# Second norm applied to the feed-forward's products, the embeddings' projection moved inside heads five to seven, and the last output column in a bank of its own

## The chip, the cores and the metric

One Trainium2 chip, one of its cores. The metric is the device time of one execution in microseconds; the kernel before takes 1887.27 us (median of three runs, 1885.65 to 1888.17).

## The reference

One encoder layer on two requests (groups 0 and 1 here) of 512 tokens and 1024 channels each, float32, with shared weights:

```
h = rmsnorm(x, g_mix);  u = h @ w_in            # -> mLSTM, attention, merge gates
y_m = (sigmoid(o) * mlstm(...)) @ w_mo
q_rope = rope(q_r, cos, sin)                     # x1*cos - x2*sin, x1*sin + x2*cos
y_a = mla_attention(q_nope, q_rope, k_nope, k_rope, v) @ w_ao     # 8 heads
x = x + (g_m * y_m + g_a * y_a) @ w_out
h2 = rmsnorm(x, g_ffn)                           # the second norm: x * r * g_ffn, r one number a token
x = x + (silu(h2 @ w_gate) * (h2 @ w_up)) @ w_down
x = x + sigmoid(x @ w_ple_gate) * (p_l @ w_ple)  # p_l: the per-layer embeddings, 256 channels
return rmsnorm(x, g_final)
```

## The kernel before

Activations lie with channels on the 128 partitions and 512 tokens along the row, so a [128, 512] tile is one block of channels of one group. A float32 product is three TensorE matmuls in a reduced format: operand and weight are each split into a rounded high part (a cast on ScalarE) and the rest (a subtraction on VectorE, `lo_of`), and hi*hi, lo*hi and hi*lo are summed in one PSUM bank. So each weight block costs TensorE three matmuls of 512 columns per 128x128, ScalarE one cast and VectorE one subtraction.

The stages, in order: norm and projections, mLSTM (to about 560 us of the profiled execution), eight attention heads, each for both groups (575 to 864 us), the chain of the mLSTM's and the attention's output projections (864 to 1019 us), the output projection `w_out` with its residual (1019 to 1111 us), sixteen projections of the embeddings (1111 to 1135 us), the feed-forward (gate and up to about 1545 us, down to 1772 us), the embedding gate and the final norm.

**Products by `Seven`.** `w_mo`, `w_ao` and the three feed-forward matrices are multiplied for both groups at once in Strassen's way: seven products (P1, P2, P7, P6, P5, Q4, P3) of twelve matmuls each stand for eight. `Ops` (L839) makes the seven operands by sums of blocks (which engine adds is its third argument), `Seven.weights` (L915) makes the sums of the weights on the engine `adds`, `outputs` (L977) combines the banks, and `chain` (L953) interleaves the products of neighbouring pairs. `put` receives each finished block.

**Attention.** `attn_proj` (L769) projects queries and keys of a head out of the low-rank latents into the PSUM tag `pj` (2 buffers, L709); every second head it also turns the rotary part with `rope` (L741): one multiply by the cosines over all 128 partitions, four multiplies by the sines over 32 partitions each, which write to exchanged partitions, and an add. `attn` (L787) does scores, softmax, transposes and the product with the values. Between the heads stand the merge gates' projections (`BULK`) in heads one to four, and the preparation of the first operands of the `w_mo` chain (`HOPS`) in heads five to seven; in its sums P7 is subtracted on VectorE, the others on GpSimd (L1014).

**Second norm.** The output projection (L1123 to L1142) works off group 0's eight columns, then group 1's. Each column's sum of squares goes into `ss`; `sums` (L1099) adds them over the partitions on TensorE (tile `ssc`), `inv` makes 1/sqrt on VectorE (tiles `rv` to `rw`), `spread2` (L1113) spreads it over the partitions again with TensorE (tile `rbc`). `hn` (L1106) multiplies a block of x with gain and norm, and the feed-forward's operands are made of those. So for group 1 the operands can only be made when the last column has been summed; meanwhile TensorE does the sixteen projections of `emb` (L1155), six matmuls each, into tiles `em` and to DRAM.

**Order.** A scheduler with a model of time orders each engine's instructions, except where `pinned` is set (the last column and `emb` here, and the end). DMAs are issued from SyncE's queue (SP), in order; those of `Seven`'s weights from ScalarE's.

Of the kernel before, what the change touches and what calls it, by code (L numbers as in the profile page):

```python
# [62 lines left out]
def encoder_kernel(ctx: ExitStack, tc: tile.TileContext, a):  # L63
# [87 lines left out]
    V.tensor_scalar(out=hg, in0=cols[:, 24:32], scalar1=0.5, scalar2=None, op0=ALU.mult)  # L151

# [588 lines left out]
    def rope(src, nblk):  # L741
        n = 32 * nblk
        r = Q("tr", "rp")
        V.tensor_tensor(out=r[0:n], in0=src[0:n], in1=cos[0:n], op=ALU.mult)
        s = Q("tr", "rs")
        for i in range(nblk):
            o = i ^ 1
            V.tensor_tensor(
                out=s[32 * o : 32 * o + 32], in0=src[32 * i : 32 * i + 32], in1=sin[32 * i : 32 * i + 32], op=ALU.mult
            )  # L750
        V.tensor_tensor(out=r[0:n], in0=r[0:n], in1=s[0:n], op=ALU.add)
        return r
# [16 lines left out]
    def attn_proj(hd, g, wa):  # L769
        if hd % 2 == 0:  # L770
            r = rope(proj1(wa, lat["cq"][g], 2, 0, "pj"), 4)
# [181 lines left out]
    def chain(quads, head=False, look=4):  # L953
# [89 lines left out]
    z1d = [[dr.tile([P, T], F32, name=f"z1d{g}_{c}") for c in range(KD)] for g in range(G)]  # L1043
# [42 lines left out]
    banks("P3", dict(mm=5, tp=1, bc=2), mm="mm", tp="ssc", bc="rbc")  # L1086
# [38 lines left out]
    pp, wple = [], []  # L1125
    w = w8("out0")
    for c in range(KD):
        nxt = w8(f"out{c + 1}") if c < KD - 1 else None
        pinned[0] = c == KD - 1
        out_proj(1, c, w, {0: lambda: sums(0), 1: lambda: spread2(0)}.get(c))  # L1130
# [3 lines left out]
        if 2 <= c < 6:
            h2.need("P1", [c - 2])
            h2.need("P2", [c - 2])
        if c == 3:
            pp = [[split(load(a[f"p{g}"][k], OP, "ev"), OP, "h", "pl") for k in range(2)] for g in range(G)]
        if c == 5:
            st = [load(a["wple"][i // 2][:, i % 2 * T : i % 2 * T + T], OP, "ev") for i in range(4)]  # L1140
            wpn[0] = 2
            wple.append(wsplit(st[0]))  # L1142


    emd = [[dr.tile([P, T], F32, name=f"emd{g}_{c}") for c in range(KD)] for g in range(G)]
    todo = [(c, g) for c in range(KD) for g in range(G)]

    emn = [0]

    def em_tile():  # L1150
        sl_, tag = ((OP, "sg"), (EV, "ch"), (OP, "sg"), (EV, "bk"))[emn[0] % 4]
        emn[0] += 1
        return sl_(tag, "em")

    def emb(n):  # L1155
        for _ in range(n):
            c, g = todo.pop(0)
            while len(wple) < min(4, c // 2 + 2):
                i = len(wple)
                wple.append(wsplit(st[i]))  # L1160
            t = em_tile()
            S.copy(t, proj1(wple[c // 2], pp[g], 2, (c % 2) * 256))
            nc.sync.dma_start(emd[g][c], t)

    emb(2)
    sums(1)
    emb(1)
    inv(1)
    emb(1)
    spread2(1)  # L1170
    emb(2)
    for k in range(4):
        h2.get("b", k)
        h2.get("d", k)
        emb((3, 3, 2, 2)[k])
    assert not todo
    pinned[0] = False
    for n in ("P7", "P6", "P3", "P5", "Q4"):
        h2.need(n)


    banks("PF", dict(b0=2, b1=3, b2=2, sp=1), b0="b0", b1="b1", b2="b2", sp="sp")
# [329 lines left out]
```

## Time and profile before

| | |
|---|---|
| median of the runs | 1887.27 us |
| profiled execution, its own time | 1886.97 us |
| its span, first to last instruction | 1885.2 us |
| TensorE busy | 1843.9 us (98%) |
| VectorE busy | 1240.2 us (66%) |
| ScalarE busy | 884.6 us (47%) |
| GpSimd busy | 371.7 us (20%) |
| mean granted TensorE clock | 0.993 |

An engine's busy time counts the durations of its instructions. Matmuls overlap: a 512-column matmul is shown with some 0.39 us, and the next one starts 0.23 us after it. What stands in square brackets behind an instruction is how long its engine was idle before it, and which instruction of which engine ended that. The granted clock is 1.0 at 2.4 GHz and 0.5 at 1.2 GHz.

### The profile page before, as it was taken

What the parts mean: (1) busy time and instruction counts of PE and PEld (TensorE: products, weight loads), DVE (VectorE), ACT (ScalarE), POOL (GpSimd) and SP (SyncE); (2) the same over time, 40 slices, a digit from 0 to 9 for tenths busy, and PEclk for the clock granted to TensorE, in tenths of its full rate; (3) what the DMA queues carried; (4) which work ended last, traced back from release to release, by engine and by line L of the source; (5) the groups of instructions that cost most, each with busy time, mean ns of one, the idle gap of its engine ahead of it and who ended that gap; (6) DMA issues with size and microseconds to landing.
All of it is one profiled execution on the core that took longest, in us unless ns stands there. A gap on an engine that the chain in (4) does not pass through costs nothing.

```text
span 1885.2 us, 24471 instructions
## 1 busy us (share of the span) xinstructions
PE 1843.9 (98%) x8849; PEld 1534.1 (81%) x8849; DVE 1240.2 (66%) x2206; ACT 884.6 (47%) x1726; POOL 371.7 (20%) x281
## 2 busy tenths in 40 slices
PE   8999999999999999899999999999999999999997
PEld 6888898988887888777877888888888887888886
DVE  6747575836554666886798487444444569878756
ACT  6255465544443665775444256333333344434433
POOL 0000000100000000242050003666466523111000
PEclk9999999999999999999999999999999999999998
DMA  4111111112253222345555342232323347543332
GB/s 166 52 45 35 57 34 57 35 67 73 79 170 129 65 73 79 123 162 181 176 196 177 102 151 79 94 130 93 102 91 106 118 144 240 158 130 109 103 129 95
DMA packets 97993, 207.59 MB, mean 110 GB/s; under 512 B 10704, under 2 KB 21328, under 8 KB 97872
## 3 DMA queue, kind: packets, MB, share of 16 engines
q1 hardware_dynamic: 85216, 161.20, 25.6%
q10 hardware_dynamic: 12096, 43.00, 7.0%
q8 instruction: 69, 1.13, 0.2%
q0 software_dynamic: 560, 1.84, 0.2%
q14 instruction: 52, 0.43, 0.1%
HBM read 151.89 MB, written 54.10 MB: 109 GB/s over the span
## 4 chain that ended last, share of the span: by engine, by line
PE 85%; DVE 9%; DMA 2%; ACT 2%; issue 1%; SPq 0%; ACTq 0%; DVEq 0%
PE b L948 12%; PE b L950 12%; PE b L949 12%; PE mm L185 8%; PE mm L183 8%; PE mm L184 8%; PE nm L633 3%; PE mm L79 3%; DVE xl L154 2%; PE mm L548 2%; PE mm L550 2%; PE mm L549 2%; DVE wp L154 1%; PE pt L812 1%; PE mm L1303 1%
## 5 line engine op out<-in xcount | busy, mean ns | idle before, releaser
L949 PE MATMUL b<-xl,wp 128*128 128x512 f32 x1148 | 447.5, 391 | 0.9 <-DVE xl L154 0.9
L948 PE MATMUL b<-xh,wp 128*128 128x512 f32 x1148 | 441.1, 392 | 6.6 <-ACT u L983 3.0
L950 PE MATMUL b<-xh,wp 128*128 128x512 f32 x1148 | 443.2, 391 | 0.6 <-DVE wp L154 0.6
L896 ACT CAST wp<-wst 128x512 fp32r<-128x512 f32 (+1 forms) x270 | 164.1, 612 | 300.9 <-PE b L950 256.5
L154 DVE TENSOR_TENSOR wp<-wst,wp 128x512 fp32r<-128x512 f32 (+1 forms) x270 | 234.7, 871 | 67.0 <-ACT wp L896 66.9
L948 PEld LDWEIGHTS b<-xh,wp 128*128 128x128 f32 x1148 | 215.6, 188 | 58.6 <-ACT u L983 6.6
L950 PEld LDWEIGHTS b<-xh,wp 128*128 128x128 f32 x1148 | 215.6, 188 | 48.2 <-DVE wp L154 1.4
L949 PEld LDWEIGHTS b<-xl,wp 128*128 128x128 f32 x1148 | 215.6, 188 | 47.9 <-DVE xl L154 1.5
L183 PE MATMUL mm<-hh,whi 128*128 128x512 f32 x560 | 220.1, 393 | 0.3 <-ACT raw L79 0.3
L184 PE MATMUL mm<-hl,whi 128*128 128x512 f32 x560 | 219.6, 392 | 0.0
L185 PE MATMUL mm<-hh,wlo 128*128 128x512 f32 x560 | 219.6, 392 | 0.0
L988 DVE TENSOR_TENSOR u<-b,u 128x512 f32<-128x512 f32 x90 | 61.5, 688 | 134.2 <-PE b L950 82.8
L168 ACT CAST whi<-wst 128x1024 fp32r<-128x1024 f32 (+1 forms) x69 | 71.0, 1028 | 116.3 <-PE mm L184 73.7
L183 PEld LDWEIGHTS mm<-hh,whi 128*128 128x128 f32 x560 | 105.6, 189 | 22.9 <-ACT raw L79 0.8
L185 PEld LDWEIGHTS mm<-hh,wlo 128*128 128x128 f32 x560 | 105.5, 188 | 21.8
L184 PEld LDWEIGHTS mm<-hl,whi 128*128 128x128 f32 x560 | 105.6, 189 | 21.5
L923 POOL TENSOR_TENSOR s<-wst,wst 128x512 f32<-128x512 f32 (+1 forms) x30 | 47.2, 1572 | 323.1 <-DMA wst<-wd 117.3
L154 DVE TENSOR_TENSOR wlo<-wst,whi 128x1024 fp32r<-128x1024 f32 (+1 forms) x69 | 83.3, 1207 | 31.2 <-ACT whi L168 30.6
L983 ACT COPY u<-b 128x512 f32<-128x512 f32 x90 | 50.8, 588 | 106.3 <-PE b L950 79.6
L1201 POOL TENSOR_TENSOR sg<-sg,u 128x512 f32<-128x512 f32 x30 | 54.9, 1831 | 216.0 <-DVE u L988 216.0
L154 DVE TENSOR_TENSOR xl<-ld,xh 128x512 fp32r<-128x512 f32 x121 | 90.3, 773 | 6.2 <-ACT xh L880 5.2
L154 POOL TENSOR_TENSOR vnl<-avt,vnh 128x512 fp32r<-128x512 f32 x16 | 21.1, 1320 | 314.2 <-ACT vnh L158 245.9
(356 smaller groups left out, 3621.0 us busy)
## 6 DMA issues: line engine op xcount, KB each, us to landing
wst<-w SPq DMA_DIRECT2D x73, 512.0 KB
wst<-w ACTq DMA_DIRECT2D x60, 512.0 KB
ld<-actd SPq DMA_DIRECT2D x77, 256.0 KB
actd<-t SPq DMA_DIRECT2D x40, 256.0 KB
x<-x SPq DMA_DIRECT2D x32, 256.0 KB
ld<-hzd SPq DMA_DIRECT2D x32, 256.0 KB
wst<-wd ACTq DMA_DIRECT2D x16, 512.0 KB
actd<-sg SPq DMA_DIRECT2D x30, 256.0 KB
```

The lines of the kernel that those rows point to most:

```text
L79: r = f(*args, **kw)
L154: e.tensor_tensor(out=out, in0=src, in1=hi.bitcast(F32), op=ALU.subtract)
L168: S.copy(hi[:, :n], st[:, :n])
L183: E.matmul(bk, whi[:, c], hi, start=k == 0, stop=False)
L184: E.matmul(bk, whi[:, c], lo, start=False, stop=False)
L185: last_mm[0] = E.matmul(bk, wlo[:, c], hi, start=False, stop=k == nk - 1)
L633: E.matmul(bk, l, r, start=n == 0, stop=n == len(terms) - 1)
L896: S.copy(hi, src)
L948: E.matmul(bk, whi[:, c], hi, start=bool(first) and k == 0, stop=False, **sk)
L949: E.matmul(bk, whi[:, c], lo, start=False, stop=False, **sk)
L950: E.matmul(bk, wlo[:, c], hi, start=False, stop=k == self.kh - 1, **sk)
L988: V.tensor_tensor(out=t, in0=b, in1=t, op=ALU.add if name == "P2" else ALU.subtract)
```

## The change

- **Norm on the products.** `Gained` replaces `hn`: the operands are made of x times gain alone, so they need no norm. `h2 @ w` comes out without its factor r, and `gate` multiplies the block with r (tile `rs2`) before and after the Silu: two more VectorE multiplies for each of the 44 gate blocks. The up block stays as it is, since its factor is the second multiply. Silu now reads SBUF always. `sums(1)`, `inv(1)` and `spread2(1)` go into the feed-forward's chain, behind its second and its fifth product. P7, P6 and P5 of each block are made within group 1's columns, which come in the order 0, 4, 1, 5, 2, 6, 3, 7.
- **Embeddings.** `emb` is called sixteen times in heads five to seven (table `EMB`), with banks of the tag `pj`; its weights are split there.
- **Last column.** It goes to a bank `lm` of its own; `mm` keeps four banks.
- **Engines.** All operand sums of the `w_mo` chain go to VectorE (P6, P5 and Q4 were on GpSimd, 16 operations), and the weight sums of two more pairs (mo 2 and ao 1, 4 operations each).
- **Rope of the first head.** One multiply by the sines over 128 partitions and four DMAs of 32 partitions each, which exchange the partitions, in place of four multiplies.
- **Final norm.** In `proj2` the small products `mid` stand before the seventh block of rows, not before the fifth.

```diff
-    def rope(src, nblk):
+    def rope(src, nblk, by_dma=False):
...
+        m = EV("ch", "rm") if by_dma else None
+        if by_dma:
+            V.tensor_tensor(out=m, in0=src, in1=sin, op=ALU.mult)
         for i in range(nblk):
...
+            f, o = slice(32 * i, 32 * i + 32), slice(32 * (i ^ 1), 32 * (i ^ 1) + 32)
+            if by_dma:
+                nc.sync.dma_start(s[o], m[f])
+            else:
+                V.tensor_tensor(out=s[o], in0=src[f], in1=sin[f], op=ALU.mult)
...
-    hops = Ops(hraw, None, lambda n: V if n == "P7" else GP)
+    hops = Ops(hraw, None, lambda n: V)
...
+        e = V if kind == "mo" and c > 1 or kind == "ao" and c < 2 else GP
...
-        e = V if (kind, c) in (("mo", 3), ("ao", 0)) else GP
...
+        t = EV("ch", "em")
+        S.copy(t, proj1(wple[i], pp[g], 2, (c % 2) * 256, "pj"))
+        nc.sync.dma_start(emd[g][c], t)
...
+            for _ in range(EMB.get((hd, g), 0)):
+                emb()
...
-    banks("P3", dict(mm=5, tp=1, bc=2), mm="mm", tp="ssc", bc="rbc")
+    banks("P3", dict(mm=4, lm=1, tp=1, bc=2), mm="mm", lm="lm", tp="ssc", bc="rbc")
...
+            if name in ("P7", "P5"):
+                t = OP("ev", "t")
+                x, c, y_ = (xd, gc, xb) if name == "P7" else (xb, ga, xa)
+                S.activation(out=t, in_=x, func=AF.Copy, scale=c)
+                V.scalar_tensor_tensor(out=t, in0=y_, scalar=ga, in1=t, op0=ALU.mult, op1=ALU.subtract)
...
+                x, c = (xa, neg[:, k : k + 1]) if name == "P6" else (xc, gc)
+                V.scalar_tensor_tensor(out=t, in0=x, scalar=c, in1=t, op0=ALU.mult, op1=ALU.add)
...
         def gate(at, t):
-            sg[at] = sg_tile()
-            S.activation(out=sg[at], in_=t, func=AF.Silu)
+            t2 = sg[at] = sg_tile()
+            V.tensor_tensor(out=t2, in0=t, in1=rs2[at[1]], op=ALU.mult)
+            S.activation(out=t2, in_=t2, func=AF.Silu)
+            V.tensor_tensor(out=t2, in0=t2, in1=rs2[at[1]], op=ALU.mult)
...
-    chain(quads, head=True)
+    def norm2():
+        sums(1)
+        inv(1)
+
+    chain(quads, head=True, beside={1: norm2, 4: lambda: spread2(1)})
...
-            if mid and k == 4:
+            if mid and k == 6:
...
+EMB = {(4, 0): 3, (4, 1): 3, (5, 0): 4, (5, 1): 4, (6, 0): 2}
```

How the order of the instructions moves, at three places. The first is VectorE at the first head's projections, where `pj` is the projected bank, `rp` and `rs` the two halves of the rope, `rm` the product that the DMAs will exchange, `wlo` a weight's low part, `qnl` and `knl` low parts of queries and keys. Before:

```order
L154 TENSOR_TENSOR wlo_5862<-wst_5858,whi_5860 128x1024
L744 TENSOR_TENSOR rp_5767<-pj_5760,cos 128x512
L748 TENSOR_TENSOR rs_5769<-pj_5760,sin 32x512 x4
L154 TENSOR_TENSOR qnl_5790<-pj_5781,qnh_5788 128x512
L751 TENSOR_TENSOR rp_5767<-rp_5767,rs_5769 128x512
L776 TENSOR_TENSOR qs_879_5775<-rp_5767,qs_879_5775 64x512
```

With the change:

```order
L156 TENSOR_TENSOR wlo_5900<-wst_5896,whi_5898 128x1024
L746 TENSOR_TENSOR rp_5801<-pj_5794,cos 128x512
L750 TENSOR_TENSOR rm_5804<-pj_5794,sin 128x512
L156 TENSOR_TENSOR qnl_5826<-pj_5817,qnh_5824 128x512
L156 TENSOR_TENSOR knl_5837<-pj_5828,knh_5835 128x512
L757 TENSOR_TENSOR rp_5801<-rp_5801,rs_5803 128x512
L746 TENSOR_TENSOR rp_5852<-pj_5845,cos 128x512
L750 TENSOR_TENSOR rm_5855<-pj_5845,sin 128x512
```

The bank is read by two instructions and no longer by five; the add waits for four DMAs, and group 1's first multiplies stand behind that add.

The second is TensorE in the fifth head: `pt` transposes, `sc` scores, `pj` a projection (from `cqh` a query's, from `plh` an embedding's). Before:

```order
L812 MATMUL pt_7546<-ident,p_7542 128x128 x4
L183 MATMUL pj_7758<-cqh_5510,whi_7656 128x512
L184 MATMUL pj_7758<-cql_5512,whi_7656 128x512
L185 MATMUL pj_7758<-cqh_5510,wlo_7658 128x512
L183 MATMUL pj_7758<-cqh_5514,whi_7656 128x512
L184 MATMUL pj_7758<-cql_5516,whi_7656 128x512
L185 MATMUL pj_7758<-cqh_5514,wlo_7658 128x512
L795 MATMUL sc_7702<-knh_7480,qnh_7469 128x512
```

With the change:

```order
L818 MATMUL pt_7665<-ident,p_7661 128x128 x4
L185 MATMUL pj_7580<-plh_7530,wp_7556 128x512
L186 MATMUL pj_7580<-pll_7532,wp_7556 128x512
L187 MATMUL pj_7580<-plh_7530,wp_7556 128x512
L185 MATMUL pj_7580<-plh_7536,wp_7556 128x512
L186 MATMUL pj_7580<-pll_7538,wp_7556 128x512
L187 MATMUL pj_7580<-plh_7536,wp_7556 128x512
L801 MATMUL sc_7855<-knh_7518,qnh_7507 128x512
```

Six matmuls that wait for no softmax stand between a head's transposes and the next scores; all sixteen such groups come before the eighth head.

The third is VectorE at the start of the feed-forward: `t` and `xl` are operands and their low parts, `wp` a weight's low part, `u` a finished block, `sg` the gate, `rv` and `ri` the start of the 1/sqrt. Before:

```order
L154 TENSOR_TENSOR xl_10956<-t_10930,xh_10954 128x512
L864 TENSOR_TENSOR hn_10555<-hn_10555,hn_10876 128x512
L988 TENSOR_TENSOR u_11048<-b_2067_11057,u_11048 128x512
L867 TENSOR_TENSOR t_10924<-t_10924,hn_10439 128x512
L154 TENSOR_TENSOR xl_10961<-t_10936,xh_10959 128x512
L154 TENSOR_TENSOR wp_11146<-wst_11030,wp_11146 128x512
```

With the change:

```order
L156 TENSOR_TENSOR wp_11119<-wst_10950,wp_11119 128x512
L156 TENSOR_TENSOR xl_10931<-t_10927,xh_10930 128x512
L997 TENSOR_TENSOR u_10970<-b_2032_10979,u_10970 128x512
L1170 SCALAR_TENSOR_TENSOR t_10927<-x_1915_10507,neg,t_10927 128x512
L156 TENSOR_TENSOR wp_11136<-wst_10952,wp_11136 128x512
L1243 TENSOR_TENSOR sg_10993<-u_10970,rs_1939_10600 128x512
L200 TENSOR_SCALAR rv_11002<-ssc_10997 128x8
L156 TENSOR_TENSOR xl_10936<-t_10927,xh_10935 128x512
L202 TENSOR_SCALAR ri_11004<-rv_11002 128x8
```

Operand sums, the gate's multiplies and group 1's 1/sqrt now stand in one queue with the weights' low parts. From the last column's residual add to the low part of the second pair's P7 weights there are 27 instructions on 512 columns and 6 on 8 columns; between the residual adds of the seventh and the eighth column there are 13 on 512 columns.


## Rows read from the trace of the kernel before

**Rows 1.** The page: busy time of each engine, share of the span and instructions.

```profile
PE 1843.9 (98%) x8849; PEld 1534.1 (81%) x8849; DVE 1240.2 (66%) x2206; ACT 884.6 (47%) x1726; POOL 371.7 (20%) x281
```

**Rows 2.** Busy time by stage (us from the start: length, then busy time and instructions of PE, PEld, DVE, ACT and POOL, granted clock, DMA share, GB/s). Heads five, six, seven and eight; the chain of `w_mo` and `w_ao`; the embeddings' projections; the first 27 us of the feed-forward; the rest of gate and up.

```profile
758.60:785.00 26.40, 25.00 (x119) 19.86 (x119) 23.15 (x48) 21.35 (x46) 10.38 (x9) 1.00 0.40 123
785.00:816.50 31.50, 25.77 (x108) 19.80 (x107) 29.56 (x59) 19.76 (x41) 6.89 (x6) 0.90 0.32 93
816.50:839.50 23.00, 22.88 (x117) 18.61 (x116) 17.86 (x41) 19.66 (x44) 7.99 (x6) 0.99 0.51 177
839.50:863.80 24.30, 20.88 (x103) 15.56 (x102) 14.34 (x34) 16.57 (x36) 12.66 (x11) 1.00 0.31 115
863.80:1019.00 155.20, 151.47 (x659) 122.94 (x658) 131.46 (x189) 69.36 (x124) 38.47 (x17) 1.00 0.58 197
...
1111.40:1135.10 23.70, 23.70 (x113) 19.78 (x112) 19.48 (x39) 15.16 (x28) 0.00 (x0) 1.00 0.42 156
1135.10:1162.00 26.90, 26.51 (x116) 21.44 (x115) 26.07 (x42) 19.54 (x35) 9.88 (x3) 1.00 0.20 69
1162.00:1545.00 383.00, 381.37 (x1663) 311.39 (x1662) 182.64 (x218) 135.07 (x235) 211.38 (x141) 1.00 0.30 104
```

**Rows 3.** Who waited for whom, TensorE alone, over the whole execution: us in total, times, longest us.

```profile
PE sc L795 <- ACT p L804: 4.5, 5, 2.4
...
PE pj L183 <- DVE rs L748: 2.5, 1, 2.5
```

**Rows 4.** TensorE in order of time at the first head's projections: start, duration, instruction, in brackets idle time before it and what ended it.

```profile
580.27 0.50 PE L183 MATMUL pj<-ckvh,whi 128*128 128x512 f32 x1 [2.51 <-DVE rs L748]
...
581.58 0.63 PE L185 MATMUL pj<-ckvh,wlo 128*128 128x512 f32 x1
...
584.14 0.63 PE L185 MATMUL pj<-cqh,wlo 128*128 128x512 f32 x1
```

**Rows 5.** VectorE there.

```profile
576.73 0.68 DVE L744 TENSOR_TENSOR rp<-pj,cos 128x512 f32<-128x512 f32 x1
577.42 2.79 DVE L748 TENSOR_TENSOR rs<-pj,sin 32x512 f32<-32x512 f32 x4
```

**Rows 6.** SyncE's queue there: one issue of a DMA.

```profile
576.83 0.33 SPq L166 DMA_DIRECT2D wst<-wa  x1
```

**Rows 7.** DMA issues: out<-in, queue, count, KB each, median us from issue to landing.

```profile
actd<-t POOLq DMA_DIRECT2D x4, 256.0 KB, 4.6
```

**Rows 8.** TensorE in order of time, head six.

```profile
789.63 0.78 PE L795 MATMUL sc<-knh,qnh 128*128 128x512 f32 x1 [2.36 <-ACT p L804]
...
791.92 0.63 PE L183 MATMUL pj<-cqh,whi 128*128 128x512 f32 x1
...
798.87 0.50 PE L795 MATMUL sc<-knh,qnh 128*128 128x512 f32 x1 [0.99 <-ACT p L804]
```

**Rows 9.** The same, a little later.

```profile
812.30 0.50 PE L821 MATMUL av<-apl,vnh 128*128 128x512 f32 x1 [1.96 <-DVE apl L154]
```

**Rows 10.** GpSimd in heads seven and eight, sums for the `w_mo` chain.

```profile
837.01 3.76 POOL L864 TENSOR_TENSOR ld<-ld,ld 128x512 f32<-128x512 f32 x3
```

**Rows 11.** TensorE in the embeddings' stage, by form: count, busy us, mean ns, idle before.

```profile
L79 PE MATMUL mm<-plh,wp 128*128 128x512 f32 x64 | 20.5, 394 | 0.0
L79 PE MATMUL mm<-pll,wp 128*128 128x512 f32 x32 | 12.5, 390 | 0.0
L79 PE MATMUL rbc<-ident,rw 128*128 128x128 f32 x8 | 1.1, 275 | 0.0
L79 PE MATMUL ssc<-onesr,sq 128*128 128x2 f32 x8 | 0.9, 240 | 0.0
```

**Rows 12.** TensorE's pace in the chain: the first matmuls of two products one behind the other.

```profile
863.71 0.39 PE L948 MATMUL b<-xh,wp 128*128 128x512 f32 x1
...
866.43 0.39 PE L948 MATMUL b<-xh,wp 128*128 128x512 f32 x1
```

**Rows 13.** VectorE in the chain of `w_mo` and `w_ao`.

```profile
952.53 1.18 DVE L154 TENSOR_TENSOR xl<-ld,xh 128x512 fp32r<-128x512 f32 x1
953.64 1.77 DVE L154 TENSOR_TENSOR wp<-wst,wp 128x512 fp32r<-128x512 f32 x1
955.33 1.77 DVE L867 TENSOR_TENSOR t<-t,ld 128x512 f32<-128x512 f32 x1
```

**Rows 14.** GpSimd there.

```profile
944.23 8.93 POOL L924 TENSOR_TENSOR wst<-wst 128x512 f32<-128x512 f32 x1
953.24 1.62 POOL L926 TENSOR_TENSOR wst<-wst,wst 128x512 f32<-128x512 f32 x1
```

**Rows 15.** VectorE in the output projection: four operations one behind the other; and the first of group 1's 1/sqrt, on 8 columns.

```profile
1100.96 2.49 DVE L154 TENSOR_TENSOR xl<-hn,xh 128x512 fp32r<-128x512 f32 x4
...
1115.15 0.17 DVE L79 TENSOR_SCALAR rv<-ssc 128x8 f32<-128x8 f32 x1 [0.90 <-PE ssc L79]
1115.36 0.17 DVE L79 TENSOR_SCALAR ri<-rv 128x8 int32<-128x8 int32 x1
```

**Rows 16.** VectorE and GpSimd in the feed-forward's gate and up stage, by form: count, busy us, mean ns, idle before.

```profile
L154 DVE TENSOR_TENSOR wp<-wst,wp 128x512 fp32r<-128x512 f32 x125 | 123.6, 989 | 49.6 <-ACT wp L896 49.6
...
L1201 POOL TENSOR_TENSOR sg<-sg,u 128x512 f32<-128x512 f32 x30 | 54.9, 1831 | 216.0 <-DVE u L988 216.0
```

**Rows 17.** TensorE at group 0's final norm.

```profile
1835.02 1.05 PE L79 MATMUL ssc<-onesr,sq 128*128 128x2 f32 x8 [0.81 <-DVE sq L268]
```

More of the change, by code (lines that the diff above doesn't have):

```diff
@@ L770, in attn_proj @@
         if hd % 2 == 0:
-            r = rope(proj1(wa, lat["cq"][g], 2, 0, "pj"), 4)
+            r = rope(proj1(wa, lat["cq"][g], 2, 0, "pj"), 4, hd == 0)
             st0 = Q("qst", "qs0", F32R)
@@ L951, in product, with chain @@
             self.out(name, self.bk)
-    def chain(quads, head=False, look=4):
+    def chain(quads, head=False, look=4, beside={}):
         order = [(0, n) for n in ("P1", "P2", "P7")]
@@ L975, in chain @@
             made[q].product(n)
+            if at in beside:
+                beside[at]()
     def outputs(put):
@@ L1027, in encoder_kernel @@
             X2 = Slots("X2", "right", x=16)
+            assert not units
             hops.r, hops.t = {}, {}
@@ L1067, in encoder_kernel @@
     oops = Ops(lambda g, k: load(ozd[g][k], X2, "x"), lambda: late["OP"]("ev", "t"), lambda n: V)
-    def pair(kind, c, ops, put):
-        e = V if (kind, c) in (("mo", 3), ("ao", 0)) else GP
-        return ops, lambda: Seven([a["w8"][W8[f"{kind}{i}"]] for i in (c, c + 4)], 4, ops, outputs(put), e)
-    chain([pair("mo", c, hops, put_z(c)) for c in range(4)] + [pair("ao", c, oops, put_y(c)) for c in range(4)])
+    chain(
+        [pair("mo", c, hops, put_z(c)) for c in range(4)] + [pair("ao", c, oops, put_y(c)) for c in range(4)],
+    )
     y = [[None] * KD for _ in range(G)]
@@ L1113, in spread2, with ffop, out_proj @@
+    def ffop(name, n, dt):
+        return (H if name in ("P1", "P2", "Q4", "P3") else OP)("h", n, dt)
+    h2 = Gained()
     def spread2(g):
-        rs2[g] = spread_f32(r2[g])
-    def out_proj(g, c, w, mid=None):
-        bk = proj1(w, y[g], mid=mid)
+        rs2[g] = H("rs", "rs2")
+        S.copy(rs2[g], spread_f32(r2[g]))
+    def out_proj(g, c, w, mid=None, bn="mm"):
+        bk = proj1(w, y[g], mid=mid, bn=bn)
         x = load(a[f"x{g}"][c], X2, "x", "x2")
@@ L1124, in encoder_kernel @@
         out_proj(0, c, w8(f"out{c}"))
-    pp, wple = [], []
     w = w8("out0")
[L1127 to L1130, printed above, removed]
+    cs = (0, 4, 1, 5, 2, 6, 3, 7)
+    for n, c in enumerate(cs):
+        nxt = w8(f"out{cs[n + 1]}") if n < KD - 1 else None
+        out_proj(1, c, w, {0: lambda: sums(0), 1: lambda: spread2(0)}.get(n), "lm" if n == KD - 1 else "mm")
         w = nxt
-        if c == 0:
+        if n == 0:
             inv(0)
[L1134 to L1182, printed above, removed]
+        if 1 <= n < 5:
+            h2.need("P1", [n - 1])
+            h2.need("P2", [n - 1])
+        if n % 2:
+            for m in ("P7", "P6", "P5"):
+                h2.need(m, [n // 2])
+    banks("PF", dict(b0=2, b1=3, b2=2, sp=1), b0="b0", b1="b1", b2="b2", sp="ssc rbc")
     actd = {}
@@ L1186, in sg_tile @@
     def sg_tile():
-        sl_, tag = ((H, "rs"), (OP, "sg"), (EV, "ch"), (OP, "sg"), (EV, "bk"))[sgn[0] % 5]
+        sl_, tag = ((OP, "sg"), (EV, "ch"), (OP, "sg"), (EV, "bk"))[sgn[0] % 4]
         sgn[0] += 1
```

89 lines of the change are left out of this document (70 added, 19 removed).

## The prediction

> **What bounds the kernel now.** The page first: TensorE is busy for 1843.9 of 1885.2 us [rows 1], so nothing gains unless it fills TensorE's idle time, restores its clock or takes matmuls away, and the change takes none away: it has the same products. Second, the windows by stage show where TensorE is not full [rows 2]: length less busy time is 1.4 us in head five, 5.7 in head six, 0.1 in seven, 3.4 in eight (10.7 together) and 3.7 in the chain of `w_mo` and `w_ao`; next to nothing in the feed-forward. In head six VectorE is busy for 29.56 of 31.5 us: there it is the bound, and the granted clock is 0.90. Third, the waits: 2.5 us for the sine products `rs` in one piece, 4.5 us in five pieces for the softmax [rows 3].
>
> The clock costs beside the gaps. After the 2.51 us wait at the first head's projections the matmuls start 0.43 us apart from 581.58 to 584.14 [rows 4], where 0.227 us is the pace (2.72 us for twelve [rows 12]): the 1.2 GHz level, for eight matmuls, 8 x 0.2 = 1.6 us. The same follows the gap of 2.36 us, and none the gap of 0.99 [rows 8]; head six's clock of 0.90 over 31.5 us is 3.2 us, which is two such stretches, the second after the gap of 1.96 [rows 2, 9].
>
> So the loss in heads five to eight is 10.7 + 3.2 = 13.9 us.
>
> **The change, part by part.** The sum is made against the profiled execution, 1886.97 us; the median lies 0.3 above it. No change measurable is 0.2%, 3.8 us.
>
> *Rope.* The four sine products take 2.79 us behind the cosine product of 0.68 [rows 5], and TensorE waits 2.51 for them. One product over 128 partitions costs what the cosine's does, 0.68 (0.60 behind another: four last 2.49 [rows 15]), so the bank is free 2.1 us earlier, the wait is 0.4, and no slow stretch follows: 2.1 + 1.6 = 3.7 us gained. The four DMAs that replace the exchange are new. Each takes 0.33 us of SyncE's queue, behind a weight's load [rows 6]; the trace has no such copy inside SBUF, so I bound one by its issue alone and by the 4.6 us of a 256 KB transfer to DRAM [rows 7]. The product is done near 578.0, the last issue starts near 579.1, so the exchanged half is there between 579.4 and 583.7. The add, and behind it group 1's two rope products, are queued on VectorE behind these DMAs: three operations, 0.60 us apart [rows 15], 1.9 us, so group 1's bank is free between 581.3 and 585.6. TensorE starts again at 578.2, and by the order does 27 matmuls before it wants that bank, 27 x 0.227 = 6.1 us: 584.3. The loss is 0 to 1.3 us, with a slow stretch to 2.9; I take 0, since a 64 KB copy is nearer the issue's end than 256 KB to DRAM is. **-3.7** (-3.7 to -0.8).
>
> *Embeddings into the heads.* 96 matmuls leave the embeddings' stage of 23.7 us [rows 2, 11] and come back in heads five to seven at 96 x 0.227 = 21.8 us. Of the 1.9 left, the small matmuls of `ssc` and `rbc` are still to be done; I put back 1.2. **-0.7** (-1.9 to 0). What counts is the fill. Six matmuls, 1.4 us, that need no softmax stand between the transposes and the next scores; their bank is emptied by ScalarE, 19.76 of 31.5 us busy. Head six gets eight such groups by the table, so TensorE there rises to 25.8 + 8 x 1.36 = 36.7 us, above VectorE's 29.6 [rows 2], and becomes the bound again. The three long gaps (2.36, 0.99, 1.96) and both slow stretches (3.2) then go: 8.5 us. Against that, VectorE gets the sums P6, P5 and Q4, 16 x 0.60 us [rows 15] = 9.6, where GpSimd took 1.25 each [rows 10]; P6's fall in heads five to seven, the others where head eight has VectorE at 14.3 of 24.3 us [rows 2]. I leave 0.5 for that. **-8** (-13.9 to 0).
>
> *Chain of `w_mo` and `w_ao`.* Eight sums of weights move from GpSimd to VectorE, which rises from 131.5 by 8 x 0.60 = 4.8, of 155.2 us [rows 2]. The trace shows both engines slowed when they run together: one GpSimd sum lasts 8.93 us while VectorE runs back to back, and beside GpSimd's next sums of 1.62 us VectorE's operations take 1.18, 1.77 and 1.77 us in place of 0.68 [rows 13, 14]. That is 2.7 us lost for a pair's four sums, against 4 x 0.6 = 2.4 for doing them on VectorE: nearly even for VectorE, but the sums come without the 8.93. TensorE is idle for 3.7 there, the most that can come back; less, since only part of it hangs on weights. **-1.5** (-3.7 to +2).
>
> The Trainium skill, "SBUF — State Buffer", section "Who interferes with whom", states more: a VectorE instruction with two SBUF inputs and a GpSimd instruction that reads SBUF share a port pair under an exclusive lock, and the loser blocks fully. Four sums would then block VectorE for 4 x 1.62 = 6.5 us, and moving them gain 6.5 - 2.4 = 4.1 a pair. The rows agree on who interferes, and 1.77 is about one GpSimd sum, but not every sum blocked one: 2.7 was lost, not 6.5, and the sum stays with that.
>
> *Start of the feed-forward.* Before, the embeddings' 23.7 us hid the norm of group 1's last column; now the products must start at once. The price of group 1's norm is off the path: the sums are behind the second product. What is late next is VectorE. Between the residual adds of the last two columns stand 13 operations on 512 columns, 13 x 0.60 = 7.8 us, where a column gives TensorE 24 x 0.227 = 5.4 [rows 12]: 2.4 behind. Then come 27 such and 6 small ones (0.2 apart [rows 15]) up to the low part of the second pair's P7 weights: 16.2 + 1.2 = 17.4, so it is ready 19.8 us after the last column. TensorE wants it after six products of 2.72 and the `ssc` matmuls, 0.9 [rows 11]: 17.2. A stall of 2.6, and 0.4 for what it does to the clock; VectorE was already at 26.07 of 26.9 us in this stretch, with 0.39 idle on TensorE [rows 2]. **+3** (0, if ScalarE's slack lets the order breathe, to +6, twice the stall and a slow stretch).
>
> *Gate.* 88 multiplies, 88 x 0.60 = 53 us, on a VectorE busy for 182.6 of 383 [rows 2]: 236, still idle for a third, so throughput hides it. The Silu waits for the first multiply and the up block for the second, a latency of 1.4 us on a block whose partner arrives products later. **+1** (0 to rival B).
>
> *Final norm.* `mid` comes two blocks of rows later, six matmuls or 1.4 us, and the wait there is 0.81 [rows 17]. **-0.8** (-0.8 to 0). The bank `lm` only lets the last column go on without the four others; nothing in the trace waits for a bank there: 0.
>
> Sum: -3.7 - 0.7 - 8 - 1.5 + 3 + 1 - 0.8 = -10.7, and 1886.97 - 10.7 = 1876.3; with the median's 0.3, **1876.6 us**.
>
> **The rivals.**
>
> *A, the projections only change place.* The waits of head six end with VectorE (the 1.96 is for `apl`), and if softmax and its low parts stay late by as much as TensorE gets work, the gaps move and remain: -10.7 + 8 = -2.7, 1884.6. For it: VectorE's 29.56 of 31.5. Against it: TensorE's load with the groups exceeds that.
>
> *B, slower: the gate's multiplies lock against GpSimd.* GpSimd does 30 multiplies `sg<-sg,u` of 1.83 us in this stage, and 125 low parts of weights already take 0.99 us there in place of 0.68 [rows 16]. The 88 new multiplies read two SBUF operands each. One that meets GpSimd loses 1.77 - 0.68 = 1.1 [rows 13]. If the delay reaches a bank that TensorE wants, it stalls 1.1. Without the gate's +1 the sum is -11.7, so it decides from 11 such stalls on (equal), and from (11.7 + 3.8) / 1.1 = 14 measurably. With half of the 44 blocks, 22: -11.7 + 24 = +12, 1899.6. Against it: VectorE is idle for a third there, and TensorE for 1.6 us in 383 in spite of 125 slowed low parts [rows 2, 16]: such delays are absorbed today. The Trainium skill's section "Who interferes with whom" speaks for this rival: by its lock each meeting would cost VectorE up to a whole GpSimd multiply of 1.83 us, as the single rows of 1.77 allow, and no row shows how often they would meet.
>
> *C, larger.* All idle time and slow stretches of heads five to seven go (7.3 + 3.2 = 10.5 in place of 8) and the feed-forward starts without a stall: -3.7 - 0.7 - 10.5 - 1.5 + 0 + 1 - 0.8 = -16.2, 1871.1.
>
> **How the numbers follow.** Forecast 0.58, A 0.17, B 0.12, C 0.13. B has the stage's absorbed delays against it; A the loads; C the count of VectorE's queue. The range reaches down past C by the chain's bound (-3.7 for -1.5 and some of the heads' rest), 1866, and up past A to no gain, 1888; B's upper end is left out, about 0.1, and a tenth is left below and between. Faster by over 0.2%: the forecast, C and a third of A, 0.76; the same: most of A and the weakest of B, 0.12; slower: B, 0.12.
>
> **What would show it.** Right: no wait over 0.6 us for the rope's bank and no half-speed matmuls near 580; head six's gaps under 1 us and its clock near 1.0, with heads five to eight about 14 us longer, not 22 (21.8 less the 8 filled); the next stage starting without 23.7 us of embeddings; one wait of 2 to 3 us for `wp` in the first six products; TensorE's idle time in gate and up still under 3 us. Wrong: a wait for the rope's add or its DMAs; gaps for `p` and `apl` as large as before; dozens of short waits for `sg`, `u` or `wp` from 1162 on.

## The result, and the profile after it

| | before | changed |
|---|---|---|
| median of 20 runs | 1884.88 us (1881.87 to 1888.17) | 1890.12 us (1885.87 to 1897.44) |
| profiled execution, its own time | 1886.97 us | 1889.58 us |
| its span | 1885.2 us | 1887.6 us |

The change makes the kernel slower: the ratio is 1.0032, 95% interval 1.0023 to 1.0041. 1876.6 us and a gain were forecast.

The page of the changed kernel answers to [rows 1]: TensorE has as much to do as before, VectorE 73 us more, GpSimd 35 less.

```profile
PE 1844.0 (98%) x8849; PEld 1533.6 (81%) x8849; DVE 1312.9 (70%) x2297; ACT 890.2 (47%) x1736; POOL 337.0 (18%) x257
```

The best view is a cut of both traces at the same instructions of TensorE, since a window by the clock mixes the stages. Each column is the time between two such starts, read from the timelines: the start of the program to the first head's first projection; to its first scores; heads one to four; five to seven; eight (its first scores to the chain's first product); the chain of `w_mo` and `w_ao`; from there to the feed-forward's first product; the feed-forward's products in fifths (the second and third together); the rest.

```
             start  rope   1-4    5-7   8      chain  to FF  FF1    FF2-3  FF4    FF5    rest
before      574.52 10.05 149.02  98.74 31.38  158.36 113.05 127.95 255.68 129.20 128.31 108.89
changed     572.55  6.37 149.52 114.21 37.41  158.58  89.30 134.23 255.44 131.74 129.59 108.67
difference   -1.97 -3.68  +0.50 +15.47 +6.03   +0.22 -23.75  +6.28  -0.24  +2.54  +1.28  -0.22
```

The first column, whose code is the same, lies between 571.8 and 576.0 us in the traces of this study: one trace can be off by 2 us there. The later stages differ less from trace to trace, but they do: where only other parts of the kernel differ, head eight varies by up to 2.2 us, the chain by up to 2.4, the feed-forward's fourth fifth by up to 2.9 and its last by up to 1.9.

**Rope.** TensorE at the first head's projections, against [rows 4]:

```profile
575.37 0.40 PE L187 MATMUL pj<-cqh,wlo 128*128 128x512 f32 x1
576.08 0.50 PE L185 MATMUL pj<-ckvh,whi 128*128 128x512 f32 x1 [0.32 <-DVE rm L750]
...
577.56 0.39 PE L185 MATMUL pj<-cqh,whi 128*128 128x512 f32 x1
...
578.92 0.84 PE L801 MATMUL sc<-knh,qnh 128*128 128x512 f32 x3
```

The wait of 2.51 us is 0.32, and no matmul runs at 1.2 GHz.

**Heads.** The windows of heads five, six, seven and eight, cut at their first scores, before and changed (columns as in [rows 2]):

```profile
733.59:770.49 36.90, 36.32 (x175) 29.68 (x174) 26.86 (x56) 25.16 (x51) 6.46 (x5) 1.00 0.42 133
770.49:803.67 33.18, 29.01 (x133) 22.89 (x132) 32.28 (x61) 24.83 (x53) 9.04 (x7) 0.95 0.34 99
803.67:832.33 28.66, 26.16 (x123) 20.50 (x122) 23.04 (x51) 21.39 (x46) 5.53 (x4) 0.94 0.31 96
832.33:863.71 31.38, 27.95 (x139) 21.37 (x138) 20.45 (x47) 22.39 (x48) 19.36 (x15) 1.00 0.47 170
```

```profile
728.44:764.72 36.28, 36.28 (x176) 29.61 (x174) 27.26 (x56) 24.95 (x51) 2.59 (x2) 1.00 0.47 144
764.72:804.62 39.90, 36.89 (x181) 29.70 (x181) 34.44 (x73) 32.72 (x69) 2.82 (x2) 1.00 0.49 150
804.62:842.64 38.02, 36.49 (x177) 29.77 (x176) 23.94 (x50) 25.23 (x53) 2.63 (x2) 1.00 0.30 105
842.64:880.05 37.41, 30.96 (x133) 22.93 (x132) 31.58 (x59) 22.49 (x47) 15.24 (x9) 0.91 0.53 183
```

The two middle heads were filled: TensorE's idle time there falls from 6.7 to 4.5 us, and the clock, which had cost some 3.4 us there (0.05 of 33.2 and 0.06 of 28.7), is back at 1.00. By the trace, two of the sixteen projections fall into head five, five into head six, eight into head seven and one into head eight, right behind its first scores at 842.64. So not all come before the eighth head, and head six got five, not the eight of the prediction. What is left in heads six and seven is mostly two waits:

```profile
802.76 0.50 PE L185 MATMUL pj<-plh,wph 128*128 128x512 f32 x1 [2.16 <-DVE qnl L156]
...
822.01 0.50 PE L185 MATMUL pj<-ckvh,whi 128*128 128x512 f32 x1 [1.53 <-DVE rs L756]
```

In the first, the filler itself waits: its bank has the tag `pj`, whose two buffers also hold the queries and keys, and those come free when VectorE has taken the low part `qnl`. The second is the four sine products of head seven's rope, which the change left as they were; it is 1.4 to 1.5 us in nine of the runs below too.

But head eight, which got one projection only, has become 6 us longer: VectorE does 31.6 us of work there where it did 20.5, TensorE's idle time is 6.5 us in place of 3.4, and the granted clock 0.91. VectorE there, 857 to 872 us (L870 are P5's sums, L876 and L877 Q4's, L807 to L815 the softmax, L156 the low parts):

```profile
857.74 0.68 DVE L870 TENSOR_TENSOR ld<-ld,ld 128x512 f32<-128x512 f32 x1
858.34 0.68 DVE L156 TENSOR_TENSOR wp<-wst,wp 128x512 fp32r<-128x512 f32 x1
858.94 0.68 DVE L870 TENSOR_TENSOR ld<-ld,ld 128x512 f32<-128x512 f32 x1
859.54 0.68 DVE L156 TENSOR_TENSOR apl<-pt,aph 128x512 fp32r<-128x512 f32 x1
860.14 1.19 DVE L870 TENSOR_TENSOR ld<-ld,ld 128x512 f32<-128x512 f32 x1
861.25 0.15 DVE L811 RECIPROCAL mx<-mx 128x1 f32<-128x1 f32 x1
...
868.21 1.28 DVE L876 TENSOR_TENSOR ld<-ld,ld 128x512 f32<-128x512 f32 x2
869.41 0.68 DVE L877 TENSOR_TENSOR ld<-ld,ld 128x512 f32<-128x512 f32 x1
870.01 0.48 DVE L815 TENSOR_SCALAR p<-p,mx 128x512 f32<-128x512 f32 x1
870.41 0.14 DVE L808 TENSOR_SCALAR mx<-mx 128x1 f32<-128x1 f32 x1
870.48 0.15 DVE L811 RECIPROCAL mx<-mx 128x1 f32<-128x1 f32 x1
```

Not one row has idle time before it. The reciprocal and the scaling that the transposes need stand between sums that nobody needs before 880. ScalarE, which scales three of four softmax blocks, waits for the reciprocal of 861.25 behind such a sum:

```profile
861.44 0.72 ACT L813 ACTIVATE p<-p,mx 128x512 f32<-128x512 f32 x1 [1.78 <-DVE mx L811]
```

TensorE waits for both:

```profile
862.74 0.63 PE L818 MATMUL pt<-ident,p 128*128 128x128 f32 x4 [1.64 <-ACT aph L820]
...
870.64 0.63 PE L818 MATMUL pt<-ident,p 128*128 128x128 f32 x4 [1.27 <-DVE mx L811]
872.56 1.91 PE L818 MATMUL pt<-ident,p 128*128 128x128 f32 x8 [1.29 <-ACT aph L820]
875.15 0.79 PE L825 MATMUL av<-aph,vnh 128*128 128x512 f32 x1 [0.68 <-ACT aph L820]
875.74 0.63 PE L826 MATMUL av<-aph,vnl 128*128 128x512 f32 x1
```

The last row begins nine matmuls 0.43 us apart: 1.2 GHz again. The granted clock is 1.00 up to 872 us and 0.50 from 873 to 879, so it fell behind the gaps of 1.27 and 1.29 us.

**Feed-forward.** The waits in its first fifth, and in the stretch where gate and up end:

```profile
1146.62 0.50 PE L954 MATMUL b<-xh,wp 128*128 128x512 f32 x1 [0.68 <-ACT wp L902]
1149.36 0.80 PE L956 MATMUL b<-xh,wp 128*128 128x512 f32 x1 [2.00 <-DVE wp L156]
...
1578.42 0.50 PE L954 MATMUL b<-xh,wp 128*128 128x512 f32 x1 [0.94 <-DVE x L1287]
1585.09 0.50 PE L954 MATMUL b<-xh,wp 128*128 128x512 f32 x1 [1.40 <-ACT wp L902]
```

The same places as windows: the clock is 0.95 in the first, and VectorE has no idle time at all in the last.

```profile
1127.93:1160.00 32.07, 29.14 (x127) 23.20 (x126) 26.77 (x50) 17.11 (x30) 4.91 (x4) 0.95 0.12 42
...
1262.16:1545.00 282.84, 281.47 (x1228) 229.85 (x1227) 190.80 (x222) 100.53 (x178) 158.78 (x103) 1.00 0.33 112
...
1560.00:1580.00 20.00, 19.07 (x84) 15.40 (x83) 20.00 (x28) 8.72 (x16) 9.33 (x9) 1.00 0.62 204
```

### The profile page after: what moved, and what is told of

Its sections match the earlier page's. It is cut to its first block, busy times and chain, and to the rows that moved or that the text cites. A ratio compares the mean times of both kernels' runs of the same rounds, so it can differ in the third digit from the quotient of the medians.

```text
span 1887.6 us, 24550 instructions
## 1 busy us (share of the span) xinstructions
PE 1844.0 (98%) x8849; PEld 1533.6 (81%) x8849; DVE 1312.9 (70%) x2297; ACT 890.2 (47%) x1736; POOL 337.0 (18%) x257
## 3 DMA queue, kind: packets, MB, share of 16 engines
q0 software_dynamic: 560, 1.84, 0.3%
## 4 chain that ended last, share of the span: by engine, by line
PE 84%; DVE 10%; DMA 2%; ACT 2%; issue 2%; SPq 0%; ACTq 0%; DVEq 0%
PE b L954 12%; PE b L956 12%; PE b L955 12%; PE mm L185 8%; PE mm L187 8%; PE mm L186 8%; PE nm L635 3%; PE mm L79 2%; DVE xl L156 2%; PE mm L550 2%; PE mm L552 2%; PE mm L551 2%; PE pt L818 1%; DVE wp L156 1%; PE pj L185 1%
## 5 line engine op out<-in xcount | busy, mean ns | idle before, releaser
L156 DVE TENSOR_TENSOR wp<-wst,wp 128x512 fp32r<-128x512 f32 (+1 forms) x272 | 239.0, 881 | 30.5 <-ACT wp L902 30.3
L156 DVE TENSOR_TENSOR wlo<-wst,whi 128x1024 fp32r<-128x1024 f32 (+1 forms) x69 | 82.2, 1191 | 30.5 <-ACT whi L170 30.1
L156 DVE TENSOR_TENSOR xl<-ld,xh 128x512 fp32r<-128x512 f32 x121 | 90.7, 775 | 10.2 <-ACT xh L886 8.4
L156 POOL TENSOR_TENSOR vnl<-avt,vnh 128x512 fp32r<-128x512 f32 x16 | 21.8, 1364 | 365.6 <-ACT vnh L160 307.5
L1249 POOL TENSOR_TENSOR sg<-sg,u 128x512 f32<-128x512 f32 x30 | 50.6, 1687 | 184.1 <-DVE rt L208 138.6
```

The costliest lines, as they stand in the source:

```text
L156: e.tensor_tensor(out=out, in0=src, in1=hi.bitcast(F32), op=ALU.subtract)
```

## The experiments

All start from the changed kernel unless it is said; a ratio is to the kernel before on the same chip (the changed kernel's is 1.0032). Theory 1 is about head eight, theory 2 about the gate's multiplies.

**1. The sums P6, P5 and Q4 on GpSimd again.**

```diff
-    hops = Ops(hraw, None, lambda n: V)
+    hops = Ops(hraw, None, lambda n: V if n == "P7" else GP)
```

> The changed kernel with one line back: the sums P6, P5 and Q4 of the operands of the w_mo chain on GpSimd again (16 operations off VectorE). Theory 1 (the fill of heads six and seven was given back in head eight, whose VectorE, busy back to back, got these sums): head eight from its first scores to the chain takes 31 to 33 us in place of 37.4, TensorE idle there 3 to 4 us in place of 6.5 and no 1.2 GHz stretch, and the whole is 4 to 6 us faster than the changed kernel's 1890.1, 1884 to 1886. Rival (the projections leave the softmax no nearer, the gaps come after them whoever makes the sums): head eight stays within 1.5 us of 37.4, the whole within 2 us of 1890.

1882.77 us, ratio 0.9983 (0.9974 to 0.9991). Head eight:

```profile
841.45:872.34 30.89, 27.50 (x134) 21.14 (x131) 24.07 (x46) 22.30 (x47) 29.92 (x22) 1.00 0.63 221
```

30.89 us, idle 3.4, clock 1.00: theory 1 as expected, the rival falls. One line was 6.5 us in head eight, and 7 us of the result by the medians. GpSimd is busy for 29.9 of 30.9 us there without making the head longer, so it is not GpSimd's work beside VectorE's that stretched it. The chain behind takes 161.15 us against 158.58; this lies within its scatter, so a small loss there is not excluded.

**2. Projections in head eight too.**

```diff
-EMB = {(4, 0): 3, (4, 1): 3, (5, 0): 4, (5, 1): 4, (6, 0): 2}
+EMB = {(4, 0): 2, (4, 1): 2, (5, 0): 3, (5, 1): 3, (6, 0): 3, (6, 1): 3}
```

> The changed kernel with the sixteen projections of the embeddings spread over heads five to eight (table 2, 2, 3, 3, 3, 3 in place of 3, 3, 4, 4, 2). Theory 1 (head eight is bound by VectorE, and has no TensorE work of its own left to do meanwhile): projections that fall into head eight fill its 6.5 us of idle time and save its slow stretch, 3 to 6 us faster than 1890.1, if VectorE's queue reaches the softmax no later. Rival (the gaps hang on VectorE's queue alone and move with it): the gaps return in heads six and seven, within 2 us of 1890.

1892.34 us, 1.0028 (1.0017 to 1.0039). The gain did not come: heads five to eight take 153.4 us against 151.6. That is the rival's time, but not its place. Heads six and seven have 0.9 and 0.7 us of idle time; the gaps stand in head eight, which by the trace has five of the projections. Its window shows that more work is no cure while VectorE is late:

```profile
834.16:881.48 47.32, 38.38 (x157) 29.75 (x156) 33.29 (x58) 24.84 (x50) 13.46 (x9) 0.82 0.48 167
```

TensorE is busy 7 us longer there and idle for 8.9 us, waits of 2.5, 3.8 and 2.0 us, at a clock of 0.82.

**3. No multiplies by the norm's factor.**

```diff
-            V.tensor_tensor(out=t2, in0=t, in1=rs2[at[1]], op=ALU.mult)
-            S.activation(out=t2, in_=t2, func=AF.Silu)
-            V.tensor_tensor(out=t2, in0=t2, in1=rs2[at[1]], op=ALU.mult)
+            S.activation(out=t2, in_=t, func=AF.Silu)
```

> The changed kernel without the 88 multiplies of the gate by the norm's factor; the output then lacks that factor. Theory 2 (they cost little in the steady part and some 3 us where gate and up end and VectorE is back to back from 1560 to 1580; and some at the start): 2 to 5 us faster than 1890.1, all of it before 1160 or after 1545, and nothing between. Rival B of the prediction (they meet GpSimd's locks): the gain lies between 1160 and 1545, and is over 5 us. If neither: within 1.5 us of 1890, and the longer waits after 1545 have another cause or are scatter of the runs.

1885.43 us, 0.9998 (0.9989 to 1.0007). The first fifth takes 131.47 us in place of 134.23, the fourth 128.75 in place of 131.74, the fifth 128.21 in place of 129.59; the second and third 255.74, no less than with the multiplies (255.44). Theory 2 holds in place, and by the medians in size (4.7 us), and rival B's place is empty. The stages add up to more, 7.1 us, but not all of it is the multiplies: in the eleven traces that have them the fourth fifth takes 130.6 to 133.5 us against 128.8 to 129.2 in the three without, while the last takes 127.7 to 129.6 us with and 128.2 to 128.8 without, so its 1.4 us is scatter. In the first 32 us the clock is 1.00, not 0.95.

**4. The rope as before** (`rope(..., 4)` without `hd == 0`).

> The changed kernel with the first head's rope as before (four sine products, no DMAs). If the rope's term was right, 3.7 us slower than the changed kernel: 1893 to 1895, with a wait of 2.5 us for the sine products and eight matmuls at 1.2 GHz. If the exchange by DMA costs elsewhere what it saves there: within 2 us of 1890.

1897.62 us, 1.0053 (1.0039 to 1.0068). The stretch to the first scores is 9.86 us in place of 6.37, with this wait and then matmuls 0.43 us apart. The term holds in that stretch (3.5 us), and for the whole by the ratios (4 us); the median lies above the range expected. Head eight, whose code is the changed kernel's, takes 35.18 us in this trace, not 37.41.

```profile
579.16 0.49 PE L185 MATMUL pj<-ckvh,whi 128*128 128x512 f32 x1 [2.52 <-DVE rs L756]
```

**5. P6 alone on VectorE** (`V if n in ("P7", "P6") else GP`).

> The changed kernel with P6's sums of the w_mo operands left on VectorE (4 operations), P5's and Q4's on GpSimd again. Theory 1 (head eight pays for VectorE's operations one by one): with 4 of the 12 sums in head eight it lies between the two runs known, 30.9 us with none and 37.4 with twelve, at 32 to 34 us, and the whole at 1884 to 1886. Rival (GpSimd's sums of weights, which run beside them in head eight and stretch VectorE's operations, are the cause, and any VectorE sum there meets them): head eight at 36 or more.

1882.17 us, 0.9986 (0.9976 to 0.9997), head eight 31.38 us. The expectation had the dose wrong: by the trace three of P6's four sums fall into the heads before and one into head eight. So it says only that one sum there costs next to nothing; it does not separate theory and rival. Runs 1 and 9 do.

**6. The gate's second multiply on GpSimd in the first and last pair** (and the edit of run 1).

```diff
-            V.tensor_tensor(out=t2, in0=t2, in1=rs2[at[1]], op=ALU.mult)
+            (GP if f1 == 0 or f2 == NF - 1 else V).tensor_tensor(out=t2, in0=t2, in1=rs2[at[1]], op=ALU.mult)
```

> The changed kernel with the sums P6, P5 and Q4 on GpSimd again, and the gate's second multiply of the first and the last pair of gate blocks on GpSimd, which has time there. Theory 2 (the gate's multiplies cost some 3 us at either end of gate and up, where VectorE is full): 1 to 4 us faster than the same kernel without that edit (1882.8), 1879 to 1882. Rival (GpSimd and VectorE slow each other there, so that nothing is won): 1882 to 1885.

1883.14 us, 0.9989 (0.9981 to 0.9998), the rival's range: nothing won against run 1. First fifth 133.05 against 133.85, fourth 131.64 against 131.25; the wait for the low part is still 1.84 us.

**7. The weight sums of mo 2 and ao 1 on GpSimd again** (and the edit of run 1).

```diff
-        e = V if kind == "mo" and c > 1 or kind == "ao" and c < 2 else GP
+        e = V if (kind, c) in (("mo", 3), ("ao", 0)) else GP
```

> The changed kernel with the sums P6, P5 and Q4 on GpSimd again, and the weight sums of mo 2 and ao 1 on GpSimd too, as before. By the prediction's term of -1.5 for moving them, 1.5 us slower than 1882.8; by the lock of the Trainium skill 4 us slower; if the weights of these pairs are never late: the same within 1 us, and the chain of w_mo and w_ao within 1 us of 158.5 to 161.

1879.51 us, 0.9974 (0.9964 to 0.9985), the fastest of all. The chain takes 160.51 us against 161.15 in run 1: neither the -1.5 nor a loss by a lock of 4 us (8 for the two pairs by the prediction's own 4.1 for each) is there. Over all traces the chain takes 158.1 to 162.1 us with these sums on VectorE and 158.4 to 160.9 with them on GpSimd, so a difference under some 2 us would not show. Whether it is faster than run 1 is not settled: the intervals overlap and the spans are 1880.3 and 1880.2.

**8. The kernel before with the rope by DMA and `mid` later, nothing else.**

> The kernel before with two edits of the change alone: the first head's rope by DMA, and the small products of the final norm before the seventh block of rows. If these two terms hold by themselves (3.7 and 0.8): 4 to 5 us faster than before's 1884.9, 1880 to 1881. If the gain in the first head is given back in the heads behind it: within 1.5 us of 1885.

1882.10 us, 0.9978 (0.9969 to 0.9987). To the first scores 6.37 us, the rest after the feed-forward 108.10 against 108.89. The wait of 0.81 us [rows 17] is gone. Both terms hold by themselves; the whole gains 4 us by the ratio.

**9. P5 on GpSimd, Q4 on VectorE** (`V if n in ("P7", "Q4") else GP`).

> The changed kernel with the sums P6 and P5 on GpSimd again and Q4's alone left on VectorE: eight of the thirteen VectorE sums that the changed kernel has in head eight. Theory 1 (head eight pays by the number of VectorE's operations there; 30.9 us with none, 37.4 with thirteen): 30.9 + 8/13 x 6.5 = 34.9, between 33.5 and 36 us. Rival (the sums made late in the head cost nothing, it is the first ones, P5's, between the weight sums of GpSimd, that delay the softmax): under 32.5 us.

1885.65 us, 1.0002 (0.9990 to 1.0014), head eight:

```profile
841.95:876.85 34.90, 29.79 (x133) 22.99 (x132) 29.95 (x54) 22.46 (x47) 21.25 (x14) 0.90 0.57 196
```

34.90 us, as worked out: none, eight and thirteen sums give 30.9, 34.9 and 37.4, 0.5 us a sum. So close a hit is luck. Without these sums head eight takes 30.8 to 32.3 us (runs 1, 6, 7, 11, 12), with thirteen 35.2 to 37.4 (run 4, run 3 and the changed kernel), so a sum costs 0.2 to 0.5 us. Runs 2 and 10, with five projections there, are left aside. Eight sums and thirteen lie above none in every trace, and the rival falls. Nor is it the sum's own 0.60 that is paid: against run 1, TensorE's idle time grows by 1.7 us, and nine matmuls run at 1.2 GHz (clock 0.90), which is another 1.8.

**10. Run 7 with the projections spread as in run 2.**

> As the run with P6, P5, Q4 and the weight sums of mo 2 and ao 1 on GpSimd (1879.5), and the embeddings' projections spread over heads five to eight. With VectorE not full in head eight any more, theory 1 expects its 3.4 us of idle time filled in part: heads five to eight together 143 to 145 us in place of 145.5, 1877 to 1880. Rival (head eight's waits are for the softmax of its last scores, which projections placed before them cannot fill): 145 to 147 us, 1879 to 1882.

1886.03 us, 0.9995 (0.9984 to 1.0006), heads five to eight 147.4 us against 145.4: the rival in place, at the edge of its range. The whole lies above both ranges; the two traces differ by 0.8 us only (spans of 1881.1 and 1880.3), so where the rest went is not shown. Head eight's last transposes still wait 1.31 and 1.46 us for VectorE's low parts of the softmax, and projections placed before them do not help.

**11. Run 7 with the first up pair's weight sums on GpSimd.**

```diff
-            e = V if f1 == 0 or f2 == NF - 1 else GP
+            e = V if f1 == 0 and kind == "fg" or f2 == NF - 1 else GP
```

> As the run with P6, P5, Q4 and the weight sums of mo 2 and ao 1 on GpSimd (1879.5), and the weight sums of the feed-forward's first up pair on GpSimd too (four operations off VectorE, back to back there from 1119 to 1148). The wait of 2.06 us for a low part of weights then shrinks by up to 4 x 0.6 = 2.4 us if VectorE's queue is the cause: 0 to 0.7 us left, the first fifth of the feed-forward's products 131.5 to 132.5 us in place of 133.8, 1877.5 to 1879. Rival (GpSimd's sums come too late or stretch VectorE's operations): 133.5 us or more.

1882.74 us, 0.9992 (0.9983 to 1.0001), first fifth 136.11 against 133.83. The wait aimed at is gone, another has grown in front of it; the expectation fails:

```profile
1130.81 1.38 PE L223 MATMUL ssc<-onesr,sq 128*128 128x2 f32 x8 [2.69 <-DVE sq L270]
1146.01 0.50 PE L956 MATMUL b<-xh,wp 128*128 128x512 f32 x1 [0.18 <-DVE wp L156]
```

**12. Run 11 with the norm two products later** (`beside={3: norm2, 5: ...}`).

> As the run with the first up pair's weight sums on GpSimd too (1882.7), and group 1's sums and 1/sqrt two products later, behind the fourth, the spread behind the sixth. In that run the wait for the low part fell from 2.06 to 0.18 us, but the wait of the sums for VectorE's last square grew from 0.39 to 2.69. Theory 2 (one full VectorE queue sets the start of the feed-forward, and a wait only moves to what is next in it until TensorE has work in front of it): both waits under 0.6 us, the first fifth of the products 131.5 to 133 us, 1877 to 1881. Rival (the wait goes on to a third place, the spread or the gate's first multiply for group 1): 133.5 us or more, 1882 or more.

1885.28 us, 0.9999 (0.9990 to 1.0008), first fifth 137.07. The rival: the wait went to a third place, the cast of a weight, in 4.15 us.

```profile
1147.68 0.80 PE L954 MATMUL b<-xh,wp 128*128 128x512 f32 x1 [4.15 <-ACT wp L902]
1150.22 0.80 PE L956 MATMUL b<-xh,wp 128*128 128x512 f32 x1 [1.32 <-DVE wp L156]
```

Runs 6, 11 and 12 did not find where VectorE's work at the feed-forward's start could go; that stays open.

## Why the prediction was wrong

Differences in us; the 21.8 us of the projections come back in the heads beside these terms.

| term | forecast | measured | by |
|---|---|---|---|
| rope | -3.7 | -3.7 | stage table, runs 4 and 8 |
| heads, fill without the sums | -8.5 | -7.2 | run 1: 144.7 against 130.1, for 21.8 added (-4.8 to -6.5 in runs 6, 7, 11 and 12) |
| heads, the sums on VectorE | +0.5 | +6.9 | changed 151.6, run 1 144.7; run 9 |
| the embeddings' old place | -23.7 | -23.8 | stage table |
| chain of `w_mo`, `w_ao` | -1.5 | +0.2 | stage table, run 7 |
| feed-forward's start, with the sums put back | +4.2 | +6.3 | stage table |
| gate behind the first fifth | +1 | +3.6 | stage table; 4.4 by run 3; 1.3 to 1.4 of either is scatter of the last fifth |
| final norm | -0.8 | -0.2 to -1.0 | the rest in the changed kernel, and in run 1 |

**The step that failed** is "I leave 0.5 for that", for the sums P6, P5 and Q4 on VectorE. I took VectorE's busy share of head eight, 14.3 of 24.3 us, as room. The share is an average: the softmax goes through VectorE one step at a time, and the thirteen sums stood between those steps in a queue that never ran empty from 843 to 872 us. Each cost 0.2 to 0.5 us, in waits of TensorE and the half-speed matmuls behind them. That head eight lacked TensorE work to stand in was not the reason: runs 2 and 10 put five projections there, and TensorE was idle for 8.9 and 5.1 us. The mechanism of the fill was right, in place and nearly in size: rival A, that the gaps only move, would have kept 21.8, and run 1 shows 14.6. It looks like rival A in the changed kernel, 21.5 us for 21.8, but the place is another: the loss came back in head eight, by another part of the change. Two premises of the fill were wrong all the same. Head six got five of the projections, not eight, and their bank is not freed by ScalarE alone, since the tag `pj` is shared: the wait of 2.16 us is a projection's. So the sign "head six's gaps under 1 us" was missed in the changed kernel; in run 1 it was met. And one of the two slow stretches that were to go is not in every execution before either: run 8 has a gap of 2.36 us in head six without it.

**The gate** was mis-sized, and at places I did not price. In the steady part, where 79 of the 88 multiplies stand, they cost nothing, as forecast (1.6 us of idle time in both kernels between 1160 and 1545), and rival B, which put its stalls there, is wrong. They cost where VectorE has no room: run 3 gives 2.8 us in the first fifth and 3.0 in the fourth, where gate and up end and the operands of the down products are made. The Trainium skill's lock ("SBUF — State Buffer", "Who interferes with whom") was cited for rival B. In the steady part 140 operations of GpSimd ran beside VectorE's, and TensorE lost nothing. The rows agree that operations with two SBUF inputs are held up. Of the gate's first multiplies in the changed kernel between 1160 and 1545 us, those that read a finished block from SBUF (`u`) take 1.06 us on average, those that read it from its bank (`b`) 0.68:

```profile
L1243 DVE TENSOR_TENSOR sg<-u,rs 128x512 f32<-128x512 f32 x29 | 30.8, 1062 | 0.0
L1243 DVE TENSOR_TENSOR sg<-b,rs 128x512 f32<-128x512 f32 x10 | 6.8, 684 | 0.0
```

So eleven of the 88, one for each four gate blocks, read one operand from SBUF and not two, as rival B took for all; and the delays of the others were not waited for. For the chain, run 7 shows no effect of either reading of it.

**The start of the feed-forward**: the stall for the second pair's P7 weights is 2.00 us where 2.6 was worked out. Counted from the feed-forward's first product (1127.93), the weights are ready after 21.4 us where I had 19.8, and TensorE wants them after 19.4 where I had 17.2. Missing from the term were the cast's wait of 0.68 and the clock, 0.95 over 32 us, which is 1.6 and not 0.4. With the 1.2 for the sums this makes 5.5 of the 6.3; the rest stays open.

**The chain** got -1.5, and no run shows a gain: its spread of 4 us over the traces, with the sums on either engine, is larger than the term.

The stage table adds up to +2.5 us, to +4.4 without its first stretch, whose code is the same; the medians say 5.2.

## What to carry to other kernels

An engine's busy share in a stage is no measure of room when the stage's critical chain runs through that engine: read its rows in order of time, and give an added instruction a price, up to its full length, wherever the queue is back to back and somebody waits at its end. When a change moves work to fill gaps, look for the stretch that the filler does not reach, keep every other added load out of it, and ask what frees the filler's own bank. Of a change of six parts test the smallest alone first: here the rope with `mid` (0.9978) brings nearly what the best mixture does (0.9974).

## What was not expected of the hardware

The four copies of 64 KB inside SBUF took little: issued from 576.05 us in 2.49 us, with VectorE's add, which waits for all four, starting at 580.17, 4.1 us after the product that they read ended.

```profile
576.05 2.49 SPq L754 DMA_DIRECT2D rs<-rm  x4
```

The length of a single gap did not decide what the clock did. Before, gaps of 2.36 and 1.96 us were each followed by matmuls at 1.2 GHz, and one of 0.99 was not [rows 8, 9]. In run 8 a gap of the same 2.36 us in head six (before 786.67) left the granted clock at 1.00. So did, in the changed kernel, one of 2.16 us (before 802.76) and one of 1.64 (before 862.74), while in head eight it fell to 0.50 near 873 us, behind gaps of 1.27 and 1.29 us with four small transposes between them, and nine matmuls of 512 columns ran at 1.2 GHz. What decides is not shown here.
